# Attention scores' third partial product on 128 rows with zeros under the keys' low part; the last matrix and the value projections move 512 weight columns

## The chip, the cores and the metric

The kernel runs on one core of a Trainium2 chip. The metric is device time in microseconds (us), as a median over runs. The engines are TensorE (PE in the profile, with its weight loads as PEld), VectorE (DVE), ScalarE (ACT), GpSimd (POOL) and SyncE (SP), which here only issues DMAs.

## The reference

The input is one sequence of 512 tokens with 1024 features. Two layers of a first block and then one layer of a second block are applied.

```python
# first block, each of 2 layers
h = rmsnorm(x, attn_norm)
a_q, a_k, a_v, b_q, b_ff, b_fb, b_i, b_g, gate_a, gate_b = split(h @ w_in)
y_a = diff_attention(a_q, a_k, a_v, ...) @ w_a     # 4 heads, 2 softmax maps of 64 dims each
y_b = hgrn2_bidirectional(b_q, ...) @ w_b          # 4 heads, gated scan over the tokens
x = x + (sigmoid(gate_a) * y_a + sigmoid(gate_b) * y_b) @ w_o
h = rmsnorm(x, ffn_norm)
x = x + (silu(h @ w_gate) * (h @ w_up)) @ w_down
# second block, 1 layer: local attention (8 heads of 64, 2 key heads), a state-space scan, and
f = square(relu(h @ w_ff_in)) @ w_ff_out           # 1024 -> 4096 -> 1024
x = x + rmsnorm(f, norm_mlp_post)
```

All values are 32-bit floats.

## The kernel before

**Products in three parts.** A large product is made from operands split into a high part (rounded to the fast 32-bit matmul type) and a low part (the rest). `mm3` (L224 to L227) issues three matmuls into the same PSUM bank: high by high, high by low, low by high. Weights come in chunks of 512 KB: `WChunk` (L203) issues one DMA on SP's queue into one of four buffers, and `wsplit` (L193) makes the parts of 512 columns when they are first used, the high part on ACT (L199), the low part on DVE (L200).

**Two orientations.** In `projA` the weights stand in the array (128 columns at a time) and all 512 tokens move through: each matmul has 512 moving columns. In `projV` (L637), which makes the values `va` and `vb` of the first block (two calls in each of two layers), and in `down` (L1538), the second block's last matrix, the tokens stand in the array, 128 at a time, and the weights move: there each matmul moves 256 weight columns. Two token tiles share one PSUM bank. `down(g)` for g = 0 to 3 takes a quarter of the 4096 hidden features each; it goes over four quarters `cq` of the output columns, for g = 3 over three, and `finish` does the last quarter token tile by token tile, with the final norm and the stores.

**Scores.** `stack_split` (L229) splits a projected query or key tile in two heads of 64 rows each. Of 128 array rows, 64 hold the high part and 64 the low part of the query (plane c of 2); for the keys both halves of plane c hold the high part, and a third plane holds the low parts of both heads. `mm_stacked` (L240) makes a pair of score tiles: for each c one matmul on 128 rows (L243: high by high plus low by high), and then for each c one on the 64 rows that hold the high parts of the query and the low parts of the keys (L246). It is called by `attn` (L719), four query tiles of each of the first block's eight heads with 512 keys, and by `local_attention` (L1174), 16 calls with 256 or 128 keys.

**Order of the work.** The Tile framework fixes each engine's order when the kernel is built: an instruction that is not ready in its planner's account is passed over and later work is taken. So in the first block matmuls of the next head's projections (`proj_h`, L680) stand in PE's order between the steps of `attn` and of `hgrn` (L760), the scan, whose levels go from PE (L775) over multiplications in `H` on POOL and DVE (L796) to a copy of the left keys on ACT (L677), and back to PE. In the second block matmuls of the gates' projections stand between the steps of the local attention.

**Where results leave PSUM.** There are three `mm` banks, two `at` banks and one each of `hg`, `tp` and `mi`. `projV` ends with eight ACT instructions (L657) of 256 columns; `down` with four a quarter, on ACT for g = 0 (L1552) and on DVE after that (L1554).

**The start.** `FirstNorm.start` (L363) issues the input's loads with the first weight chunks of `projV` between them.

Of the kernel before, what the change touches and what calls it, by code (L numbers as in the profile page):

```python
# [11 lines left out]
F32 = mybir.dt.float32  # L12
# [59 lines left out]
def model_kernel(ctx: ExitStack, tc: tile.TileContext, I, O, dbg=None):  # L72
# [155 lines left out]

    def stack_split(src, dst):  # L229

        keys = dst.shape[1] == 3
        for c in range(2):
            own, other = slice(c * 64, c * 64 + 64), slice(64 - c * 64, 128 - c * 64)
            A.activation(out=dst[own, c, :], in_=src[own, :], func=AF.Copy)
            if keys:
                A.activation(out=dst[other, c, :], in_=src[own, :], func=AF.Copy)
            V.tensor_tensor(out=dst[own, 2, :] if keys else dst[other, c, :], in0=src[own, :], in1=dst[own, c, :],
                            op=ALU.subtract)

    def mm_stacked(pss, q, k):  # L240

        for c in range(2):
            PE.matmul(out=pss[c], lhsT=q[:, c, :], rhs=k[:, c, :], start=True, stop=False)  # L243
        for c in range(2):
            own = slice(c * 64, c * 64 + 64)
            PE.matmul(out=pss[c], lhsT=q[own, c, :], rhs=k[own, 2, :], start=False, stop=True)  # L246

    def projA(W, c0, nm, xsf, K=8, kbase=0, loader=None, hooks=None):

# [71 lines left out]
    class Norm:  # L321
# [8 lines left out]
        def on(self, m, x):  # L330
            sc = {} if self.pre is None else {"scale": self.pre[:, m:m + 1]}
            if self.n == 0:
                A.activation(out=self.ss, in_=x, func=AF.Square, **sc)
            else:
                sq = stile([128, 512], "sq", bufs=2)
                A.activation(out=sq, in_=x, func=AF.Square, **sc)  # L336
                if self.n < 7 or not self.short:
                    P.tensor_tensor(out=self.ss, in0=self.ss, in1=sq, op=ALU.add)  # L338
                else:
                    self.parts.append(sq)  # L340
            self.n += 1
# [18 lines left out]
    class FirstNorm:  # L360


        def start(self, ah, va, vb, Win):  # L363
            self.xt = [ah.tile([128, 4, 512], F32, name="H4", tag="H4", bufs=2) for _ in range(2)]
            self.xm = [va[:, m, :] for m in range(4)] + [vb[:, m, :] for m in range(4)]
            self.ah, pre = ah, {}
            for q in range(4):
                nc.sync.dma_start(out=self.xt[q // 2][:, :, q % 2 * 256:q % 2 * 256 + 256],
                                  in_=I["x"][0, :, q * 256:q * 256 + 256].rearrange("(t p) c -> p t c", p=128))
                if q % 2 == 0:  # L370
                    pre[(0, q // 2)] = WChunk(Win, 0, 4, 1024 + q // 2 * 256, 256)

            wm = ah.tile([128, 512], F32, name="e", tag="e", bufs=3)
            V.memset(wm, 0.0)
            A.activation(out=wm[0:1, 0:1], in_=mhalf[0:1, 0:1], func=AF.Copy)
            gps = mi_ps()
            for _ in range(WARM):
                PE.matmul(out=gps[:, 0:256], lhsT=wm[:, 128:256], rhs=wm[:, 256:512], start=True, stop=True)
            PE.transpose(gps[:, 0:8], prow0, ident[0:8, 0:8])
            self.g0 = stile([128, 8], "g0", bufs=1)  # L380
            V.tensor_copy(out=self.g0, in_=gps[:, 0:8])
            for m in range(4):
                self.tile(m)
                if m % 2:
                    pre[(0, 0)](m - 1, slice(0, 256))
            return pre

        def tile(self, m):
# [242 lines left out]
    def heads(l, Win, nrm, oA, oB, op_, ah):  # L631
# [3 lines left out]
        vb = ah.tile([128, 4, 512], F32, name="vb")  # L635

        def projV(c0, dst, hooks=None, pre={}):  # L637
            banks = [[mm_ps(), mm_ps()], [mm_ps(), at_ps()]]
            for k0 in (0, 4):
                for cc in range(2):  # L640
                    pss = banks[cc]
                    w = pre.get((k0, cc)) or WChunk(Win, k0, 4, c0 + cc * 256, 256)
                    for ka in (0, 2):
                        for t in range(4):
                            o = pss[t // 2][:, (t % 2) * 256:(t % 2) * 256 + 256]
                            for k in (ka, ka + 1):
                                xh, xl = xs(k0 + k)
                                ts_ = slice(t * 128, (t + 1) * 128)
                                wh, wl = w(k, slice(0, 256))
                                mm3(o, xh[:, ts_], xl[:, ts_], wh, wl,  # L650
                                    k0 + k == 0 and t % 2 == 0, k0 + k == 7 and t % 2 == 1)
                    if hooks is not None:
                        next(hooks, None)
            rcol = nrm.cols
            for cc in range(2):
                for t in range(4):
                    A.activation(out=dst[:, t, cc * 256:cc * 256 + 256],  # L657
                                 in_=banks[cc][t // 2][:, (t % 2) * 256:(t % 2) * 256 + 256],
                                 func=AF.Copy, scale=rcol[:, t:t + 1])

        def proj_rope(c0, tag):
            mark("proj_" + tag)
# [4 lines left out]
            V.tensor_tensor(out=t1, in0=ps, in1=Crs, op=ALU.mult)  # L667
            P.tensor_tensor(out=sh, in0=sh, in1=Srs, op=ALU.mult)
            V.tensor_tensor(out=t1, in0=t1, in1=sh, op=ALU.add)
            dst = ah.tile([128, 2 if tag == "aq" else 3, 512], F32R, name=tag, tag=tag, bufs=2)  # L670
            stack_split(t1, dst)
            return dst

# [500 lines left out]
    def local_attention(lp, oL, kvp):  # L1174
# [17 lines left out]
        pad(lp, 992)  # L1192
        kt = lp.tile([128, 512], F32, name="kt", tag="kt", bufs=1)
        V.tensor_tensor(out=kt, in0=kvp[0], in1=rbc, op=ALU.mult)
        kh = lp.tile([128, 3, 512], F32R, name="kh")
        stack_split(kt, kh)
        vt = lp.tile([128, 512], F32, name="vt", tag="kt", bufs=1)
        V.tensor_tensor(out=vt, in0=kvp[1], in1=rbc, op=ALU.mult)
# [116 lines left out]
    with ExitStack() as mst:  # L1315
# [78 lines left out]
        with ExitStack() as st:  # L1394
# [20 lines left out]
                            m == 0 and k == 0, m == 1 and k == 7)  # L1415

            def evac(hs, p, ps):
                sq = stile([128, 512], "sq", bufs=2)
                A.activation(out=sq, in_=ps[p], func=AF.Square)
                for j in range(2):  # L1420
                    A.activation(out=yo[:, 4 + 2 * p + j, hsl(hs)], in_=ps[p][:, hsl(j)], func=AF.Copy,
                                 scale=gpost[4 + 2 * p + j])
                ss = pn.ss[:, hsl(hs)]
                if p == 1:
                    return [ss, sq[:, hsl(0)], sq[:, hsl(1)]]
                for j in range(2):
                    P.tensor_tensor(out=ss, in0=ss, in1=sq[:, hsl(j)], op=ALU.add)
# [55 lines left out]
    with ExitStack() as st:  # L1483
# [50 lines left out]
        def squares(t, cq):  # L1534
            jk = fp.tile([128, 256], F32, name="jk", tag="jk", bufs=2)
            A.activation(out=jk, in_=acc[:, t, cq * 256:cq * 256 + 256], func=AF.Square, accum_out=ssq[:, t, cq:cq + 1])

        def down(g):  # L1538
            for cq in range(4 if g < 3 else 3):
                pss = [mm_ps() for _ in range(2)]  # L1540
                csl = slice(cq * 256, cq * 256 + 256)
                for k0 in (0, 4):
# [5 lines left out]
                for t in range(4):  # L1548
                    o = pss[t // 2][:, (t % 2) * 256:(t % 2) * 256 + 256]
                    dst = acc[:, t, csl]  # L1550
                    if g == 0:
                        A.activation(out=dst, in_=o, func=AF.Copy, scale=r2[:, t:t + 1])  # L1552
                    else:
                        V.scalar_tensor_tensor(out=dst, in0=o, scalar=r2[:, t:t + 1], in1=dst, op0=ALU.mult, op1=ALU.add)  # L1554
# [77 lines left out]
```

## Time and profile before

| | us |
|---|---|
| median of 3 runs (2378.78 to 2381.04) | 2378.87 |
| the profiled execution | 2378.16 |
| its span on the core | 2376.4 |
| PE busy, share of the span | 2340.1, 98% |
| PEld busy | 1967.3, 83% |
| DVE busy | 1366.8, 58% |
| ACT busy | 1030.5, 43% |
| POOL busy | 448.2, 19% |

The profile is of one execution, 0.7 us under the median. 1.8 us of it lie outside the span. A matmul's duration in the rows includes the time in which its results leave the array, while the next one already runs: what one matmul costs is read from the distance between two starts and not from its duration. In a row of the timeline the columns are start, duration, engine, line, operation, tiles and shape, how many instructions are merged, and in brackets the engine's idle time before it with what ended that.

### The profile page before, as it was taken

How to read it: one execution, taken by the hardware profiler on the slowest of the kernel's cores; microseconds unless marked ns; L12 is line 12 of the kernel's file. 1: busy time of each engine (PE TensorE's matmuls, PEld its weight loads, DVE VectorE, ACT ScalarE, POOL GpSimd, SP SyncE). 2: the span in 40 equal slices, each digit the busy share in tenths (PEclk: the TensorE clock that was granted, in tenths of full speed). 3: DMA queues.
4: the chain of work that ended last, by engine and by line, in shares of the span. 5: the costliest groups of instructions: out<-in, count | busy, mean ns of one | idle time of the engine just before them, and what ended most of it. 6: DMA issues, size and time to landing. Idle time of an engine off the chain costs nothing.

```text
span 2376.4 us, 32220 instructions
## 1 busy us (share of the span) xinstructions
PE 2340.1 (98%) x12207; PEld 1967.3 (83%) x12207; DVE 1366.8 (58%) x2370; ACT 1030.5 (43%) x1936; POOL 448.2 (19%) x754
## 2 busy tenths in 40 slices
PE   9999999999999999999999999999999999999998
PEld 9877788888888897777888888888776788898998
DVE  5777755554444547777556544445766875434444
ACT  6566644433232335566434332323356354533232
POOL 0122210170151311222101726100300102000002
PEclk9999999999999999999999999999999999999999
DMA  6211124333333432111243333333433543233231
GB/s 224 71 54 54 54 71 160 106 103 105 106 101 106 130 116 72 54 48 60 66 131 106 110 113 106 107 107 92 125 97 107 169 142 98 83 96 98 89 98 63
DMA packets 252539, 237.53 MB, mean 100 GB/s; under 512 B 18936, under 2 KB 237640, under 8 KB 252384
## 3 DMA queue, kind: packets, MB, share of 16 engines
q1 hardware_dynamic: 232992, 204.81, 28.4%
q10 hardware_dynamic: 15584, 21.33, 2.8%
q0 software_dynamic: 3808, 9.33, 1.3%
q8 instruction: 96, 1.57, 0.3%
q14 instruction: 59, 0.48, 0.1%
HBM read 216.42 MB, written 20.59 MB: 100 GB/s over the span
## 4 chain that ended last, share of the span: by engine, by line
PE 87%; DVE 7%; ACT 2%; issue 2%; DMA 1%; POOL 1%; ACTq 0%; DVEq 0%; POOLq 0%
PE mm L225 24%; PE mm L227 24%; PE mm L226 24%; PE hg L775 2%; PE at L246 1%; PE at L243 1%; DVE hT L800 1%; PE at L227 1%; PE at L225 1%; PE at L226 1%; DVE wlo L200 1%; PE mi L750 1%; PE tp L744 1%; PE hg L1254 1%; POOL H L796 0%
## 5 line engine op out<-in xcount | busy, mean ns | idle before, releaser
L200 DVE TENSOR_TENSOR wlo<-wraw,whi 128x512 fp32r<-128x512 f32 x736 | 536.6, 733 | 706.3 <-ACT whi L199 683.3
L199 ACT ACTIVATE whi<-wraw 128x512 fp32r<-128x512 f32 x736 | 458.6, 629 | 891.6 <-PE mm L226 665.3
L225 PE MATMUL mm<-xg,whi 128*128 128x512 f32 (+1 forms) x1736 | 679.8, 392 | 1.6 <-DVE dt L905 1.6
L226 PE MATMUL mm<-xg,whi 128*128 128x512 f32 (+1 forms) x1736 | 676.3, 390 | 1.3 <-DVE xg L1436 1.2
L227 PE MATMUL mm<-xg,wlo 128*128 128x512 f32 (+1 forms) x1736 | 676.4, 390 | 0.0
L227 PEld LDWEIGHTS mm<-xg,wlo 128*128 128x128 f32 x1736 | 326.7, 188 | 69.4 <-issue 4.8
L225 PEld LDWEIGHTS mm<-xg,whi 128*128 128x128 f32 x1736 | 327.0, 188 | 67.9 <-issue 3.4
L226 PEld LDWEIGHTS mm<-xg,whi 128*128 128x128 f32 x1736 | 327.0, 188 | 67.8 <-issue 2.7
L226 PE MATMUL mm<-wlo,a 128*128 128x256 f32 x512 | 144.9, 283 | 0.0
L227 PE MATMUL mm<-whi,a 128*128 128x256 f32 x512 | 144.9, 283 | 0.0
L225 PE MATMUL mm<-whi,a 128*128 128x256 f32 x512 | 144.9, 283 | 0.0
L225 PE MATMUL mm<-a,whi 128*128 128x512 f32 x352 | 137.2, 390 | 0.6 <-DVE dt L905 0.6
L226 PE MATMUL mm<-a,whi 128*128 128x512 f32 x352 | 136.9, 389 | 0.0
L227 PE MATMUL mm<-a,wlo 128*128 128x512 f32 x352 | 136.9, 389 | 0.0
L338 POOL TENSOR_TENSOR ss<-ss,sq 128x512 f32<-128x512 f32 x36 | 54.1, 1510 | 372.3 <-ACT sq L336 371.6
L796 POOL TENSOR_TENSOR H<-H,hT 128x512 f32<-128x512 f32 x56 | 65.2, 1165 | 225.6 <-PE hg L775 148.1
L225 PEld LDWEIGHTS mm<-whi,a 128*128 128x128 f32 x512 | 98.3, 192 | 0.1
L226 PEld LDWEIGHTS mm<-wlo,a 128*128 128x128 f32 x512 | 98.3, 192 | 0.1
L227 PEld LDWEIGHTS mm<-whi,a 128*128 128x128 f32 x512 | 98.3, 192 | 0.0
L225 PEld LDWEIGHTS mm<-a,whi 128*128 128x128 f32 x352 | 66.1, 188 | 14.9 <-DVE dt L905 1.0
L227 PEld LDWEIGHTS mm<-a,wlo 128*128 128x128 f32 x352 | 66.1, 188 | 13.7
L226 PEld LDWEIGHTS mm<-a,whi 128*128 128x128 f32 x352 | 66.1, 188 | 13.7
(491 smaller groups left out, 3829.5 us busy)
## 6 DMA issues: line engine op xcount, KB each, us to landing
wraw<-in_w_in_dram SPq DMA_DIRECT2D x118, 512.0 KB, 3.7
wraw<-in_w_gate_dram SPq DMA_DIRECT2D x44, 512.0 KB, 3.6
wraw<-in_w_up_dram SPq DMA_DIRECT2D x44, 512.0 KB, 3.8
wraw<-in_w_down_dram SPq DMA_DIRECT2D x40, 512.0 KB, 3.4
wraw<-in_w_ff_in_dram SPq DMA_DIRECT2D x32, 512.0 KB, 3.7
wraw<-in_w_ff_out_dram SPq DMA_DIRECT2D x32, 512.0 KB, 3.4
wraw<-in_w_o_dram SPq DMA_DIRECT2D x16, 512.0 KB, 3.6
xT<-xd SPq DMA_DIRECT2D x24, 256.0 KB, 5.0
```

The source lines that it names most:

```text
L199: A.activation(out=hi[:, :n], in_=raw, func=AF.Copy)
L200: V.tensor_tensor(out=lo[:, :n], in0=raw, in1=hi[:, :n], op=ALU.subtract)
L225: PE.matmul(out=ps, lhsT=ah, rhs=bh, start=first, stop=False)
L226: PE.matmul(out=ps, lhsT=ah, rhs=bl, start=False, stop=False)
L227: PE.matmul(out=ps, lhsT=al, rhs=bh, start=False, stop=last)
L243: PE.matmul(out=pss[c], lhsT=q[:, c, :], rhs=k[:, c, :], start=True, stop=False)
L246: PE.matmul(out=pss[c], lhsT=q[own, c, :], rhs=k[own, 2, :], start=False, stop=True)
L338: P.tensor_tensor(out=self.ss, in0=self.ss, in1=sq, op=ALU.add)
L744: PE.transpose(tp[:, b * 128:(b + 1) * 128], es[0][:, b * 128:(b + 1) * 128], ident)
L750: PE.matmul(out=o[:, i * 128:(i + 1) * 128], lhsT=wT[:, b * 128:(b + 1) * 128], rhs=va[:, b, h * 128:(h + 1) * 128], start=b == 0, stop=b ...
L775: PE.matmul(out=ps[:, sl].rearrange("p (n two h) -> p n two h", two=2, h=hh), lhsT=KT[:, sl], rhs=halves(H4, 1, 2, hh, b * 128, 128), star ...
L796: eng.tensor_tensor(out=tgt, in0=tgt, in1=mul.unsqueeze(3).to_broadcast([128, 2, nb, hh]), op=ALU.mult)
```

## The change

1. `stack_split` gives the keys four planes. Plane 2 + c holds the low part of head c on its own 64 rows, and zeros on the other 64, written by a `memset` on POOL (two for each of the nine key tiles).
2. `mm_stacked` makes the third product on 128 rows, right behind the first one of the same c, with the same stationary tile.
3. The scratch tile `sq` of the norms moves from the pool that lives through the kernel to the pool of the residual stream; the two key buffers of the first block are 2 KB larger each.
4. `projV` moves 512 columns: chunks of two rows of tiles by 512 columns (512 KB, as before), one PSUM bank for each token tile, four ACT instructions of 512 columns at the end. `FirstNorm.start` loads the first two of these chunks at the same places in the queue.
5. `down(0)` to `down(2)` and the first half of `down(3)` move 512 columns (`down_half`): columns 0 to 511 into the banks `at`, `at`, `tp`, `mi`, columns 512 to 1023 into the three `mm` banks and `hg`. The third quarter of `down(3)` and `finish` stay as they were.

```diff
     def stack_split(src, dst):
-        keys = dst.shape[1] == 3
+        keys = dst.shape[1] == 4
...
             if keys:
                 A.activation(out=dst[other, c, :], in_=src[own, :], func=AF.Copy)
-            V.tensor_tensor(out=dst[own, 2, :] if keys else dst[other, c, :], in0=src[own, :], in1=dst[own, c, :],
+                P.memset(dst[other, 2 + c, :].bitcast(F32), 0.0)
+            V.tensor_tensor(out=dst[own, 2 + c, :] if keys else dst[other, c, :], in0=src[own, :], in1=dst[own, c, :],
                             op=ALU.subtract)
     def mm_stacked(pss, q, k):
         for c in range(2):
             PE.matmul(out=pss[c], lhsT=q[:, c, :], rhs=k[:, c, :], start=True, stop=False)
-        for c in range(2):
-            own = slice(c * 64, c * 64 + 64)
-            PE.matmul(out=pss[c], lhsT=q[own, c, :], rhs=k[own, 2, :], start=False, stop=True)
+            PE.matmul(out=pss[c], lhsT=q[:, c, :], rhs=k[:, 2 + c, :], start=False, stop=True)
...
-                sq = stile([128, 512], "sq", bufs=2)
+                sq = cur["xp"].tile([128, 512], F32, name="sq", tag="sq", bufs=2)
...
-                    pre[(0, q // 2)] = WChunk(Win, 0, 4, 1024 + q // 2 * 256, 256)
+                    pre[q] = WChunk(Win, q, 2, 1024, 512)
...
         def projV(c0, dst, hooks=None, pre={}):
-            banks = [[mm_ps(), mm_ps()], [mm_ps(), at_ps()]]
-            for k0 in (0, 4):
-                for cc in range(2):
...
+            banks = [mm_ps(), mm_ps(), mm_ps(), at_ps()]
+            for k0 in range(0, 8, 2):
+                w = pre.get(k0) or WChunk(Win, k0, 2, c0, 512)
+                for k in range(2):
+                    xh, xl = xs(k0 + k)
+                    wh, wl = w(k, slice(0, 512))
+                    for t in range(4):
+                        ts_ = slice(t * 128, (t + 1) * 128)
+                        mm3(banks[t], xh[:, ts_], xl[:, ts_], wh, wl, k0 + k == 0, k0 + k == 7)
+                if hooks is not None:
+                    next(hooks, None)
...
+            for t in range(4):
+                A.activation(out=dst[:, t, :], in_=banks[t], func=AF.Copy, scale=rcol[:, t:t + 1])
...
+        def down_half(g, ch):
+            pss = [at_ps(), at_ps(), tp_ps(), mi_ps()] if ch == 0 else [mm_ps(), mm_ps(), mm_ps(), hg_ps()]
+            csl = slice(ch * 512, ch * 512 + 512)
+            for k0 in range(0, 8, 2):
+                w = WChunk(W2, g * 8 + k0, 2, ch * 512, 512)
+                for k in range(2):
+                    for t in range(4):
...
+                        mm3(pss[t], a[:, 0, tsl], a[:, 1, tsl], wh, wl, k0 + k == 0, k0 + k == 7)
+            for t in range(4):
+                evac(g, t, csl, pss[t])
...
         def down(g):
-            for cq in range(4 if g < 3 else 3):
+            down_half(g, 0)
+            if g < 3:
+                down_half(g, 1)
+                return
+            for cq in (2,):
```

## Rows read from the trace of the kernel before

**Rows 1.** The page's first part: busy time, share and instructions of an engine.
```profile
PE   2340.1 (98%) x12207; PEld 1967.3 (83%) x12207; DVE 1366.8 (58%) x2370; ACT 1030.5 (43%) x1936; POOL 448.2 (19%) x754
```

**Rows 2.** Groups by line and shape on PE: columns as in the page's part 5.
```profile
L225 PE MATMUL mm<-whi,a 128*128 128x256 f32 x512 | 144.9, 283 | 0.0
...
L225 PE MATMUL mm<-whi,xg 128*128 128x256 f32 x192 | 54.5, 285 | 0.1
...
L225 PE MATMUL at<-whi,xg 128*128 128x256 f32 x64 | 18.1, 283 | 0.0
```

**Rows 3.** Timeline of PE in `down(0)`, 256 moving columns.
```profile
2110.23 0.28 PE L225 MATMUL mm<-whi,a 128*128 128x256 f32 x1
...
2111.19 0.28 PE L227 MATMUL mm<-whi,a 128*128 128x256 f32 x1
```

**Rows 4.** Timeline of PE in the projection after it, 512 moving columns.
```profile
2150.22 0.39 PE L225 MATMUL mm<-xg,whi 128*128 128x512 f32 x1
...
2150.90 0.39 PE L225 MATMUL mm<-xg,whi 128*128 128x512 f32 x1
```

**Rows 5.** The 64-row matmuls by shape: one line's view.
```profile
L246 PE MATMUL at<-ak,aq x64: 491/498/502, 92.6 to 1129.7; 64*128 64x512 f32 x64
...
L246 PE MATMUL at<-kh,qh x32: 322/380/384, 1745.9 to 1804.6; 64*128 64x256 f32 x24, 64*128 64x128 f32 x8
```

**Rows 6.** Timeline of PE: a scores call whose 64-row matmuls stand alone.
```profile
218.61 0.39 PE L243 MATMUL at<-ak,aq 128*128 128x512 f32 x1
218.92 0.50 PE L246 MATMUL at<-ak,aq 64*128 64x512 f32 x1
219.35 0.50 PE L225 MATMUL mm<-xg,whi 128*128 128x512 f32 x1
219.69 0.39 PE L243 MATMUL at<-ak,aq 128*128 128x512 f32 x1
```

**Rows 7.** Timeline of PE: a call whose two 64-row matmuls stand together.
```profile
225.34 0.94 PE L243 MATMUL at<-ak,aq 128*128 128x512 f32 x2
226.21 0.50 PE L246 MATMUL at<-ak,aq 64*128 64x512 f32 x2
226.65 0.50 PE L227 MATMUL mm<-xg,wlo 128*128 128x512 f32 x1
```

**Rows 8.** Timeline of PE: the first call of a head.
```profile
212.18 0.50 PE L243 MATMUL at<-ak,aq 128*128 128x512 f32 x1 [0.31 <-DVE aq L237]
212.90 0.50 PE L243 MATMUL at<-ak,aq 128*128 128x512 f32 x1 [0.22 <-DVE aq L237]
```

**Rows 9.** Timeline of PE: a call of the local attention, 256 keys.
```profile
1760.26 0.28 PE L243 MATMUL at<-kh,qh 128*128 128x256 f32 x1
...
1761.74 0.27 PE L1249 MATMUL tp<-ident,lg 128*128 128x128 f32 x1
```

**Rows 10.** Timeline of ACT: copies of the left keys in a head's scan.
```profile
231.72 0.62 ACT L677 COPY hKT<-H 128x512 f32<-128x512 f32 x1 [1.47 <-DVE amx L732]
...
239.57 0.62 ACT L677 COPY hKT<-H 128x512 f32<-128x512 f32 x1 [1.31 <-DVE arc L738]
```

**Rows 11.** Timeline of PE: the scan's matmuls that read those copies.
```profile
232.64 1.05 PE L775 MATMUL hg<-H,hKT 128*128 128x128 f32 x8
```

**Rows 12.** The same, without a scores call since the level before.
```profile
240.24 1.16 PE L775 MATMUL hg<-H,hKT 128*128 128x128 f32 x8 [0.18 <-ACT hKT L677]
```

**Rows 13.** Windows: L225 alone, a head's stretch with its scan; PE busy and count first.
```profile
213.76:249.18 35.42, 8.36 (x20) 3.78 (x20) 1.00 0.15 46
```

**Rows 14.** POOL, groups by shape: one input, 512 columns.
```profile
L1045 POOL TENSOR_SCALAR Z<-BA,cf 128x512 f32<-128x512 f32 x8 | 12.6, 1589 | 0.4
```

**Rows 15.** A `memset` of 512 columns on DVE, one line's view.
```profile
L374 DVE MEMSET e<- x1: 485/485/485, 1.2 to 1.2; 128x512 f32 x1
```

**Rows 16.** DVE, groups by shape: a result of 512 columns read from PSUM.
```profile
L394 DVE SCALAR_TENSOR_TENSOR xg<-at,g,xg 128x512 fp32r<-128x512 f32 x2 | 1.5, 748 | 1.1 <-ACT xg L393 1.1
```

**Rows 17.** Timeline of ACT where layer 1's first `projV` ends.
```profile
34.62 1.28 ACT L438 ACT_TABLE_LOAD   x1
```

More of the change, by code (lines that the diff above doesn't have):

```diff
@@ L384, in start @@
                 if m % 2:
-                    pre[(0, 0)](m - 1, slice(0, 256))
+                    pre[0](m // 2, slice(0, 512))
             return pre
@@ L637, in projV @@
         def projV(c0, dst, hooks=None, pre={}):
-            banks = [[mm_ps(), mm_ps()], [mm_ps(), at_ps()]]
-            for k0 in (0, 4):
-                for cc in range(2):
[L641 to L653, printed above, removed]
-            rcol = nrm.cols
[L655 to L659, printed above, removed]
+            banks = [mm_ps(), mm_ps(), mm_ps(), at_ps()]
[9 more added lines that the diff above has]
+                    next(hooks, None)
+            rcol = nrm.cols
+            for t in range(4):
+                A.activation(out=dst[:, t, :], in_=banks[t], func=AF.Copy, scale=rcol[:, t:t + 1])
         def proj_rope(c0, tag):
@@ L669, in proj_rope @@
             V.tensor_tensor(out=t1, in0=t1, in1=sh, op=ALU.add)
-            dst = ah.tile([128, 2 if tag == "aq" else 3, 512], F32R, name=tag, tag=tag, bufs=2)
+            dst = ah.tile([128, 2 if tag == "aq" else 4, 512], F32R, name=tag, tag=tag, bufs=2)
             stack_split(t1, dst)
@@ L1194, in local_attention @@
         V.tensor_tensor(out=kt, in0=kvp[0], in1=rbc, op=ALU.mult)
-        kh = lp.tile([128, 3, 512], F32R, name="kh")
+        kh = lp.tile([128, 4, 512], F32R, name="kh")
         stack_split(kt, kh)
@@ L1417, in evac @@
             def evac(hs, p, ps):
-                sq = stile([128, 512], "sq", bufs=2)
+                sq = cur["xp"].tile([128, 512], F32, name="sq", tag="sq", bufs=2)
                 A.activation(out=sq, in_=ps[p], func=AF.Square)
@@ L1536, in squares, with evac @@
             A.activation(out=jk, in_=acc[:, t, cq * 256:cq * 256 + 256], func=AF.Square, accum_out=ssq[:, t, cq:cq + 1])
-        def down(g):
-            for cq in range(4 if g < 3 else 3):
+        def evac(g, t, csl, o):
+            dst = acc[:, t, csl]
+            if g == 0:
+                A.activation(out=dst, in_=o, func=AF.Copy, scale=r2[:, t:t + 1])
+            else:
+                V.scalar_tensor_tensor(out=dst, in0=o, scalar=r2[:, t:t + 1], in1=dst, op0=ALU.mult, op1=ALU.add)
+        def down_half(g, ch):
[5 more added lines that the diff above has]
+                    for t in range(4):
+                        a = acts[g * 8 + k0 + k]
+                        tsl = slice(t * 128, (t + 1) * 128)
+                        wh, wl = w(k, slice(0, 512))
+                        mm3(pss[t], a[:, 0, tsl], a[:, 1, tsl], wh, wl, k0 + k == 0, k0 + k == 7)
+            for t in range(4):
+                evac(g, t, csl, pss[t])
+                if g == 3:
+                    for cq in (2 * ch, 2 * ch + 1):
+                        squares(t, cq)
+                    P.tensor_tensor(out=acc[:, t, csl], in0=acc[:, t, csl], in1=gpb[:, csl], op=ALU.mult)
+        def down(g):
+            down_half(g, 0)
[3 more added lines that the diff above has]
+            for cq in (2,):
                 pss = [mm_ps() for _ in range(2)]
@@ L1550, in down @@
                     dst = acc[:, t, csl]
[L1551 to L1554, printed above, removed]
+                    evac(g, t, csl, o)
                     if g == 3:
```

## The prediction

> **What bounds the kernel now.** I read the page's first part, then PE's groups by shape, then PE's timeline. The page shows PE busy 98% of the span with more weight loads and matmuls than any engine has instructions [rows 1]. So the question for each edit is what it does to the distance between PE's starts, and whether PE then waits for something else. The timeline gives that distance, since a duration covers the way out of the array too. A matmul of 256 moving columns follows the one before it after 0.120 us: 8 steps from 2110.23 to 2111.19 [rows 3]. One of 512 takes 0.227: 3 steps in 0.68 [rows 4]. Two narrow ones cost 0.240, one wide one 0.227: each instruction costs 13 ns beside its columns.
>
> The second thing to see is what happens around a 64-row matmul. There are 96: 64 with 512 columns, 24 with 256, 8 with 128 [rows 5]. Where one stands alone, it starts 0.31 us after the 128-row matmul before it, the next one 0.43 after that, and the one after that 0.34 later [rows 6]. At 0.227 each, three steps are 0.68; they take 1.08. So 0.40 us is lost at each. The Trainium skill, "TensorEngine Tiling (Array Packing)", section "Key Properties", says that changing the tiling mode, not just the tile, drains the engine; the trace agrees, by those 0.40 us.
>
> **Part A, 512 weight columns.** The narrow matmuls of `down` are 512 in each of three forms, those of `projV` 192 + 64 in each [rows 2], so 1536 and 768. Of `down`'s, 96 stay for the third quarter of g = 3 and 96 in `finish`. 1344 + 768 = 2112 become 1056, and each pair gives 13.3 ns (0.240 less 0.68/3): 14.1 us. Columns, high and low splits and their work on ACT and DVE stay the same, and so do the number, size and place of the weight DMAs on SP's queue; a split of 512 columns now serves 12 matmuls of 0.227 (2.72 us) instead of 24 of 0.120 (2.88 us), so it must come 6% sooner.
>
> What can take some of it back is the end of a group. Before, half of the banks were done half a group early; now four banks are done in the last 2 us, 0.68 us apart, and the next projection wants the first at once and the second 1.36 us later. This happens at six places: after four `projV` calls (ACT) and after `down(0)` and `down(1)` (DVE). The first bank is done 2.04 us before the group's end and read in about 0.75 us [rows 16], so 1.3 us are left for whatever stands before it on that engine. The worst thing seen there is a table load of 1.28 us on ACT, behind the end of the first `projV` [rows 17]. The bound is 0 to 1.3 us for each; I take 0.25, nearer to nothing since one such load just fits: 1.5 us. Part A nets 12.6 us. The half of `down(3)` goes into banks that nobody wants after it, and the end of the kernel (third quarter, `finish`) is not touched: nothing.
>
> **Part B, scores on 128 rows.** In the first block each head has four calls. In two of them the 64-row matmuls stand alone, as in [rows 6]: 8 heads with 4 alone, 32 in all, at 0.40: 12.8 us. In the other two calls of a head they stand together, and these two run beside each other: both begin at about 226.21, and the next instruction starts 0.44 later [rows 7], which is no less than two wide matmuls one after the other (0.453). The drain before (0.31 less 0.227, 0.09) and the load after (0.34 less 0.227, 0.11) remain, less the 0.01: 0.19 for each of 16 pairs, 3.0 us. At the first call of a head the second matmul waits for the query's split, 0.72 us behind the first [rows 8]; in the new order the third product of c = 0 lies in that wait: 0.227 for 8 heads, 1.8 us. Heads: 17.6 us.
>
> In the local attention a call with 256 keys takes from 1760.26 to 1761.74, with one projection matmul in it [rows 9]: 1.48 against 4 x 0.120 + 0.227 = 0.71. That is 0.77 for 12 calls, 9.2 us. The four calls with 128 keys I estimate between a pair (0.19) and this (0.77), at 0.4: 1.6 us. Local: 10.8. Part B gross: 28.4 us.
>
> How much arrives? Freed PE time is lost if the next instruction in PE's fixed order waits for another chain. In the scan, a copy of the keys ends at 231.72 + 0.62 = 232.34 [rows 10] and PE reads it at 232.64 [rows 11]: 0.30 us to spare, with one lone 64-row matmul (0.40) since the level before. At a level without a call the copy ends at 240.19 and PE is there at 240.24 [rows 10, 12]: it waits for it. So the spare time is about what the calls cost PE, and without that cost PE comes just in time rather than early. I charge 0.3 us a head, 2.4, and in the local attention, whose chains over DVE and ACT are denser, a quarter, 2.7 (between nothing and all 10.8; my choice, as most of its steps have projection matmuls in front). Part B nets 23.3 us.
>
> **Small edits.** Two POOL memsets for each of nine key tiles, 64 x 512: a row of 512 columns costs 0.49 us on DVE [rows 15] and at most 1.6 on POOL [rows 14]; so 1 to 3.2 us a head on POOL. Behind them on POOL stand the query's rotation and the scan's multiplications. They are covered since the keys are made one projection (24 x 0.227 = 5.4 us) before the query, and the memset waits for no data. If that cover failed, a head would lose up to 3.2 us (26 in all, in the range's upper end in part). The scratch tile `sq` moves 4 KB without adding an instruction: nothing. The loads at the start keep size and place: nothing.
>
> **Sum.** Profiled execution 2378.16 (span 2376.4 and 1.8 outside) less 12.6 less 23.3 is 2342.3; the median lies 0.7 above the profiled one: 2343.
>
> **Rivals.** (1) *The freed time in the calls is waited out.* The order on PE stays, and the scan's and the softmax's chains set the pace. For it: PE waits already at levels without a call [rows 12]. Against it: the spare time before the others [rows 10, 11]. With three quarters of part B lost: 2378.9 - 12.6 - 7.1 = 2359. (2) *The 64-row products were cheap.* A pair of them works in the array at once, and two products on 128 rows replace one slot by two. If the gaps around them were due to something that stays, 32 pairs at 0.227, 12 at 0.120 and 4 at some 0.11 would be added, 9.1 us: 2378.9 - 12.6 + 9.1 = 2375. The same page of the Trainium skill, in "When to Use Tiling", advises two-fold row tiling for a contraction of 64, and so speaks against this change; the trace speaks against the rule here, since a pair takes 0.44. (3) *The order gets worse, and it is slower.* In a head's 35 us of scan some 60 projection matmuls (20 from each of three lines) stand between the chain's steps [rows 13]. The order is made anew at each build. If a third of them fell out of that stretch (20 x 0.227 = 4.5 us a head, 36 in all), by three wide banks held longer or by memsets ahead of the scan, the whole gain would be gone, and with half of them it is 2378.9 - 35.9 + 54 = 2397. Nothing in the rows points there, but nothing excludes it.
>
> **How the numbers follow.** The forecast has 0.80, with its own range of 2334 (all of A and B, 42.5 less, and a little more) to 2353; rival 1 has 0.12, rival 2 has 0.03, rival 3 has 0.05. The range reaches from 2334 to rival 1's 2360. About 0.2% (4.8 us) is what a measurement here can tell from no change. Faster: forecast and rival 1, 0.92. Same: rival 2, 0.03. Slower: rival 3, 0.05.
>
> **What would show it.** In the profile after, `down` and `projV` should show L225 to L227 with 512 columns, 0.227 us apart, and 1056 fewer matmuls. L246 should be gone, and in a call four starts 0.227 apart, with the next matmul at 0.227 too. Wrong would be: steps of 0.3 or more in these calls (rival 2); idle time before L775, L744 or L1249 that was not there (rival 1); fewer projection matmuls in a head's scan (rival 3); a wait for ACT or DVE at the first matmul behind `projV` or `down` of more than 1.3 us; a wait for POOL before the scores.

## The result and the profile after

The changed kernel takes 2349.71 us (median of 4, 2348.67 to 2351.14), the kernel before 2378.82 us beside it: a ratio of 0.9877 (95% interval 0.9860 to 0.9894). That is 29.1 us less; the sum had 35.9. The time lies in the range, and the sign and the likeliest case came true, but one term of the sum was wrong by ten microseconds.

The profile after has a span of 2347.3 us, 29.1 less than before. Part 1 of its page, against [rows 1]:

```profile
PE 2301.5 (98%) x11151; PEld 1912.0 (81%) x11151; DVE 1369.9 (58%) x2350; ACT 1029.2 (44%) x1912; POOL 460.1 (20%) x768
```

PE has 1056 matmuls fewer (12207 less 11151), as counted, and its share still reads 98%: the share doesn't tell that something new is waited for. The groups by shape, which answer to [rows 2]:

```profile
L225 PE MATMUL mm<-whi,xg 128*128 128x512 f32 x96 | 38.2, 398 | 0.4 <-ACT whi L199 0.4
...
L225 PE MATMUL mm<-whi,a 128*128 128x512 f32 x72 | 28.0, 389 | 0.0
...
L225 PE MATMUL mm<-whi,a 128*128 128x256 f32 x64 | 18.1, 283 | 0.0
```

What is left of 256 columns in `down` is the third quarter of g = 3 and `finish`. The view of the first score line, which answers to [rows 5] (L245 has the same shapes and counts):

```profile
L244 PE MATMUL at<-ak,aq x64: 389/474/504, 89.5 to 1120.4; 128*128 128x512 f32 x64
...
L244 PE MATMUL at<-kh,qh x32: 220/282/387, 1735.8 to 1785.7; 128*128 128x256 f32 x24, 128*128 128x128 f32 x8
```

Its last row gives the length of the local attention's scores, 1735.8 to 1785.7. In [rows 5] it is 1745.9 to 1804.6: nine of the 29 us lie there. The other stages were measured in the same way, from the start of one matmul to the start of another in PE's timeline of either kernel:

| stage | before | after | difference | gross in the prediction |
|---|---|---|---|---|
| `projV`, layer 1 (its first to its last matmul) | 49.03 | 46.53 | -2.50 | -2.55 |
| heads, layer 1 (first scores to first `w_a` matmul) | 251.99 | 249.68 | -2.31 | -8.8 |
| `projV`, layer 2 | 48.23 | 47.54 | -0.69 | -2.55 |
| heads, layer 2 | 254.54 | 251.59 | -2.95 | -8.8 |
| local attention (first to last scores) | 58.94 | 49.96 | -8.98 | -10.8 |
| first `down` matmul to the end | 278.38 | 269.39 | -8.99 | -8.94 |
| all the rest | 1435.3 | 1432.6 | -2.7 | 0 |

So the loss is in the heads: 5.3 us arrived of 17.6. The scores calls there did become what was planned. PE's timeline in a head, which answers to [rows 6]:

```profile
213.48 0.39 PE L244 MATMUL at<-ak,aq 128*128 128x512 f32 x1
213.71 0.39 PE L245 MATMUL at<-ak,aq 128*128 128x512 f32 x1
213.93 0.39 PE L225 MATMUL mm<-xg,whi 128*128 128x512 f32 x1
214.16 0.39 PE L244 MATMUL at<-ak,aq 128*128 128x512 f32 x1
214.39 0.39 PE L245 MATMUL at<-ak,aq 128*128 128x512 f32 x1
214.62 1.13 PE L766 MATMUL hg<-H,hKT 128*128 128x128 f32 x8
```

All starts are some 0.23 us apart. (From `projV` on, lines are 9 lower than before: L775 is now L766, L744 is L735, L739 is L730, L796 is L787.) What changed beside that stands in the view of PE's waits for the stretch from 100 to 300 us, three and a third heads. Its columns are what waited for what, us in total, times, the longest. First the kernel before, then the changed one:

```profile
PE at L243 <- DVE aq L237: 2.2, 6, 1.0
PE hg L809 <- POOL H L796: 1.5, 3, 0.8
PE hg L775 <- ACT hKT L677: 0.5, 3, 0.2
```

```profile
PE tp L735 <- DVE e L732: 5.2, 8, 1.1
PE at L244 <- DVE aq L238: 2.2, 3, 1.1
PE hg L766 <- ACT hKT L668: 1.9, 8, 0.3
PE hg L774 <- DVE H L787: 1.1, 4, 0.3
```

4.2 us of waits became 10.4. The new one is the first: the transposes of the softmax weights (L735) wait for VectorE's combination of the two maps (L732), up to 1.1 us once in a head. One such place in the changed kernel, on DVE, POOL and PE:

```profile
219.97 0.17 DVE L729 RECIPROCAL arc<-als 128x2 f32<-128x2 f32 x1 [1.37 <-ACT e L725]
220.18 0.99 DVE L730 TENSOR_TENSOR arc<-arc,nlam 128x1 f32<-128x1 f32 x1
221.09 0.72 DVE L768 COPY_PREDICATED hWd<-cm,hg 128x512 f32<-128x512 uint8 x1
221.70 0.73 DVE L732 SCALAR_TENSOR_TENSOR e<-e,arc 128x512 f32<-128x512 f32 x1
...
219.99 1.16 POOL L787 TENSOR_TENSOR H<-H,hT 128x512 f32<-128x512 f32 x1 [2.65 <-ACT e L725]
...
219.60 0.47 PE L244 MATMUL at<-ak,aq 128*128 128x512 f32 x1
...
222.58 0.63 PE L735 MATMUL tp<-ident,e 128*128 128x128 f32 x4 [1.10 <-DVE e L732]
```

L730 multiplies one number in each partition. It takes 0.99 us, begins 0.19 us behind a multiplication of the scan on POOL, and ends with it (221.17 and 221.15). Beside no POOL instruction it takes 0.15. In the kernel before the same instruction stands later against POOL's:

```profile
225.74 1.16 POOL L796 TENSOR_TENSOR H<-H,hT 128x512 f32<-128x512 f32 x1 [2.62 <-ACT e L734]
...
225.76 0.17 DVE L738 RECIPROCAL arc<-als 128x2 f32<-128x2 f32 x1 [1.37 <-ACT e L734]
225.84 0.74 DVE L777 COPY_PREDICATED hWd<-cm,hg 128x512 f32<-128x512 uint8 x1
226.48 0.43 DVE L739 TENSOR_TENSOR arc<-arc,nlam 128x1 f32<-128x1 f32 x1
...
227.44 0.74 DVE L741 SCALAR_TENSOR_TENSOR e<-e,arc 128x512 f32<-128x512 f32 x1
...
228.32 0.63 PE L744 MATMUL tp<-ident,e 128*128 128x128 f32 x4
```

There it again ends with POOL's (226.91 and 226.90), but only 0.42 us of that were left. Both happen in 8 of the 32 calls, once in each head. The Trainium skill, "SBUF — State Buffer", section "SBUF: two separate sides", says that VectorE and GpSimd share one pair of ports as an exclusive lock: a VectorE instruction with two inputs in SBUF and a GpSimd instruction that reads SBUF don't run beside each other, and the later one stands still until the first has ended. The trace agrees, by 0.99 and 0.43 against 0.15 us.

The longer L730 does not make this chain longer, however. From the start of the reciprocal to the end of the combination it takes 2.42 us in the kernel before (225.76 to 228.18) and 2.46 in the changed one (219.97 to 222.43), as VectorE does its work there in another order. What changed is PE. Before, it comes to the transposes 0.14 us behind the combination, after the two 64-row products and six projection matmuls; in the changed kernel it has had no 64-row products and only three projection matmuls to do there (the others stand elsewhere), and is idle for 1.10 us. From the first matmul of the scores call that stands before them to the transposes it is 2.98 us in both (from 225.34 in [rows 7], and from 219.60).

### The profile page after: what moved, and what is told of

Same layout as the page of the kernel before. It is cut to its first block, busy times and chain, and to the rows that moved or that the text cites. A ratio compares the mean times of both kernels' runs of the same rounds, so it can differ in the third digit from the quotient of the medians.

```text
span 2347.3 us, 30081 instructions
## 1 busy us (share of the span) xinstructions
PE 2301.5 (98%) x11151; PEld 1912.0 (81%) x11151; DVE 1369.9 (58%) x2350; ACT 1029.2 (44%) x1912; POOL 460.1 (20%) x768
## 4 chain that ended last, share of the span: by engine, by line
PE 82%; DVE 10%; ACT 3%; issue 3%; DMA 1%; POOL 1%; ACTq 0%; DVEq 0%; POOLq 0%
PE mm L225 22%; PE mm L226 22%; PE mm L227 22%; DVE H L787 2%; PE hg L766 1%; PE at L225 1%; PE at L227 1%; PE at L226 1%; DVE hWd L768 1%; DVE e L732 1%; DVE hT L791 1%; DVE wlo L200 1%; ACT hKT L668 1%; PE at L244 1%; PE hg L225 1%
## 5 line engine op out<-in xcount | busy, mean ns | idle before, releaser
L225 PE MATMUL mm<-xg,whi 128*128 128x512 f32 (+1 forms) x1736 | 678.7, 391 | 1.6 <-DVE dt L896 1.6
L225 PEld LDWEIGHTS mm<-xg,whi 128*128 128x128 f32 x1736 | 327.2, 188 | 66.4 <-DVE dt L896 2.0
L225 PE MATMUL mm<-a,whi 128*128 128x512 f32 x352 | 137.2, 390 | 0.6 <-DVE dt L896 0.6
L787 POOL TENSOR_TENSOR H<-H,hT 128x512 f32<-128x512 f32 x56 | 66.8, 1193 | 217.9 <-PE hg L766 122.4
L225 PEld LDWEIGHTS mm<-a,whi 128*128 128x128 f32 x352 | 66.1, 188 | 14.8 <-DVE dt L896 1.0
L227 PEld LDWEIGHTS mm<-a,wlo 128*128 128x128 f32 x352 | 66.1, 188 | 13.8
L225 PE MATMUL mm<-mrg,whi 128*128 128x512 f32 (+1 forms) x208 | 75.9, 365 | 0.0
L226 PE MATMUL mm<-mrg,whi 128*128 128x512 f32 (+1 forms) x208 | 75.8, 365 | 0.0
L227 PE MATMUL mm<-mrg,wlo 128*128 128x512 f32 (+1 forms) x208 | 75.8, 365 | 0.0
L766 PEld LDWEIGHTS hg<-H,hKT 128*128 128x128 f32 x448 | 59.1, 191 | 12.7 <-ACT hKT L668 10.6
L1553 POOL TENSOR_TENSOR acc<-acc,gpb 128x512 f32<-128x512 f32 x4 | 5.5, 1406 | 322.4 <-ACT jk L1527 322.4
L766 PE MATMUL hg<-H,hKT 128*128 128x128 f32 x448 | 64.8, 288 | 3.7 <-ACT hKT L668 3.7
```

What stands on the lines that cost most here:

```text
L225: PE.matmul(out=ps, lhsT=ah, rhs=bh, start=first, stop=False)
L226: PE.matmul(out=ps, lhsT=ah, rhs=bl, start=False, stop=False)
L227: PE.matmul(out=ps, lhsT=al, rhs=bh, start=False, stop=last)
L766: PE.matmul(out=ps[:, sl].rearrange("p (n two h) -> p n two h", two=2, h=hh), lhsT=KT[:, sl], rhs=halves(H4, 1, 2, hh, b * 128, 128), star ...
L787: eng.tensor_tensor(out=tgt, in0=tgt, in1=mul.unsqueeze(3).to_broadcast([128, 2, nb, hh]), op=ALU.mult)
```

## The experiments

The theory after these readings: in the heads the chains of the softmax and the scan over VectorE and ScalarE come last, not PE; the 64-row matmuls stood in time in which PE would otherwise have waited; and VectorE's instructions that stand still beside GpSimd's make these chains long. The rivals: the 64-row matmuls were cheap; the two parts of the change hinder each other; the new order alone is at fault.

**One part alone: the 512 columns.** The changed kernel with the three-plane keys and the 64-row products of before.

```diff
...
-            PE.matmul(out=pss[c], lhsT=q[:, c, :], rhs=k[:, 2 + c, :], start=False, stop=True)
+        for c in range(2):
+            own = slice(c * 64, c * 64 + 64)
+            PE.matmul(out=pss[c], lhsT=q[own, c, :], rhs=k[own, 2, :], start=False, stop=True)
...
```

> The changed kernel with the scores as they were (64-row third products, keys in three planes); only the 512 weight columns are new. By the trace of the changed kernel, the stages with wide weights gave 2.4 us in layer 1's value projections, 0.7 in layer 2's and 9.0 in the last matrix. Theory (both parts are independent): 12 us less than before, 2367. Rival (part of the loss in the heads comes from the wide projections, whose order the planner changed as well): under 2364 or over 2370, with head periods other than before's 60 to 61 us.

Measured: 2364.79 us (2362.83 to 2366.48), ratio 0.9942 (0.9925 to 0.9959): 13.8 us less than before. Part A gives its 14.1 gross nearly whole.

**The other part alone: the 128-row scores.** The kernel before with the new `stack_split`, `mm_stacked` and `sq`, and 256 columns in `projV` and `down`.

```diff
...
-        for c in range(2):
-            own = slice(c * 64, c * 64 + 64)
-            PE.matmul(out=pss[c], lhsT=q[own, c, :], rhs=k[own, 2, :], start=False, stop=True)
+            PE.matmul(out=pss[c], lhsT=q[:, c, :], rhs=k[:, 2 + c, :], start=False, stop=True)
...
```

> The kernel before with the scores' third product on 128 rows and nothing else (the scratch tile sq moves with it, for room). Theory: the local attention gives about 10.8 us, the eight heads only 4 to 6 of the 17.6 us that the 64-row products cost there, since PE then waits for the softmax and the scan: 2362 to 2364. Rival (the heads lost their gain through the wide projections): 2350 to 2353.

Measured: 2363.25 us (2361.40 to 2365.46), ratio 0.9937 (0.9922 to 0.9951): 15.4 us less. 13.8 and 15.4 are 29.2, the changed kernel has 29.1: the parts don't hinder each other. The multiplication of one number takes 0.99 to 1.00 us in eight calls here too, and 0.43 to 0.44 in the run before, with the old scores: it comes with part B.

**64 rows again, in the order of after.** Every engine's instructions stand as in the changed kernel; only the third product reads its own 64 rows.

```diff
-            PE.matmul(out=pss[c], lhsT=q[:, c, :], rhs=k[:, 2 + c, :], start=False, stop=True)
+            own = slice(c * 64, c * 64 + 64)
+            PE.matmul(out=pss[c], lhsT=q[own, c, :], rhs=k[own, 2 + c, :], start=False, stop=True)
```

> The changed kernel with its order of issue in the scores, its four key planes and its memsets, but the third product reads only the 64 rows of its head. Theory (a change between 128 and 64 rows drains the array, 0.40 us for each of 96 products that stand alone): in the local attention some 10 us more, in the heads less than the 64 x 0.40 = 26 us because PE waits there anyway; 2362 to 2380. Rival (64-row products are cheap, the order made the gain): 2346 to 2353.

Measured: 2372.33 us (2370.14 to 2374.56), ratio 0.9975 (0.9965 to 0.9985), 22.6 us over the changed kernel. In this order the 64-row form costs 13.5 us in the heads and 9.7 in the local attention. In the heads some 2.6 us of that are two stretches of lower granted clock (an estimate, from the lengths of heads with and without one; see the end), so 10.9: the products were not cheap. But all 64 of them stand alone in this order, each between two matmuls of 128 rows, and at the prediction's 0.40 us each that would be 25.6. The place shown above, in PE's timeline of this run (it is 5.72 us later in the span):

```profile
225.32 0.48 PE L244 MATMUL at<-ak,aq 128*128 128x512 f32 x1
225.74 0.49 PE L246 MATMUL at<-ak,aq 64*128 64x512 f32 x1
226.16 0.50 PE L244 MATMUL at<-ak,aq 128*128 128x512 f32 x1
226.59 0.50 PE L246 MATMUL at<-ak,aq 64*128 64x512 f32 x1
227.02 0.50 PE L225 MATMUL mm<-xg,whi 128*128 128x512 f32 x1
...
228.30 0.63 PE L736 MATMUL tp<-ident,e 128*128 128x128 f32 x4 [0.32 <-DVE e L733]
```

From the first scores matmul to the transposes it is 228.30 - 225.32 = 2.98 us, with two 64-row products alone and a wait of 0.32. In the changed kernel it is 222.58 - 219.60 = 2.98 us, with none and a wait of 1.10. Here part B gained nothing: the chain over VectorE sets the end, and the time around the 64-row products stood in its shadow. The small multiplication takes 1.12 to 1.14 us here, longer than in the changed kernel, and PE waits less.

With 64 rows the heads are 8.2 us longer in this order than in the kernel before, 5.6 without the stretches of lower clock. That is no sign that the order of the other engines got worse: in the kernel before 32 of the products stand alone and 32 in 16 pairs, 15.8 us at the prediction's prices against the 25.6 here, and PE's waits over both layers' heads add up to 12 us there, 13 here and 23 in the changed kernel.

**The small multiplication with one input from a tile.** L730 takes `nlam` as a scalar operand.

```diff
-                V.tensor_tensor(out=r[:, 1:2], in0=r[:, 1:2], in1=nlam[:, l:l + 1], op=ALU.mult)
+                V.tensor_scalar(out=r[:, 1:2], in0=r[:, 1:2], scalar1=nlam[:, l:l + 1], scalar2=None, op0=ALU.mult)
```

> The changed kernel; the multiplication of the softmax's second reciprocal by minus lambda (one number a row, line 730 in the changed kernel) reads lambda as a scalar operand, so that the VectorE instruction has one tensor input, not two. In the changed kernel it took 0.99 us where it began 0.2 us behind a GpSimd multiplication and ended with it, against 0.15 us alone, and the transposes that need its result made PE wait 1.28 us in each head. Theory (two tensor inputs on VectorE wait for GpSimd's tensor instruction): it takes 0.2 us everywhere, the wait at line 735 falls by about 0.85 us a head, and the time by 4 to 7 us, to 2343 to 2346. Rival (the wait is the chain of the softmax itself): it still takes 0.9 us or PE waits as long in another place, 2349 to 2351.

Measured: 2346.90 us (2345.89 to 2347.09), ratio 0.9867 (0.9852 to 0.9881): 2.8 us less than the changed kernel, a little short of what was expected. The instruction takes 0.20 to 0.22 us in all calls. But the order came out otherwise, and it no longer stands behind POOL's multiplication; that this form doesn't stand still is not shown. PE's waits from 100 to 300 us:

```profile
PE hg L800 <- POOL H L787: 2.3, 3, 0.8
PE at L244 <- DVE aq L238: 2.0, 3, 1.0
PE hg L774 <- DVE H L787: 1.3, 4, 0.3
PE tp L735 <- DVE e L732: 1.2, 4, 0.3
PE hg L766 <- ACT hKT L668: 0.8, 4, 0.2
```

The wait at L735 fell from 5.2 to 1.2, and the scan's own last level (L800) is late now instead: 7.6 us remain of 10.4.

**The softmax's scale later.** The first map is scaled at the output, four ACT instructions a head, and VectorE makes the ratio of the two maps in one instruction.

```diff
...
-                V.tensor_tensor(out=r[:, 1:2], in0=r[:, 1:2], in1=nlam[:, l:l + 1], op=ALU.mult)
-                A.activation(out=es[0], in_=es[0], func=AF.Copy, scale=r[:, 0:1])
+                V.tensor_scalar(out=r[:, 1:2], in0=r[:, 1:2], scalar1=ls[:, 0:1], scalar2=nlam[:, l:l + 1],
+                                op0=ALU.mult, op1=ALU.mult)
...
-            A.copy(out=oA[:, h, :], in_=o)
+            for i in range(4):
+                A.activation(out=oA[:, h, i * 128:i * 128 + 128], in_=o[:, i * 128:i * 128 + 128], func=AF.Copy,
+                             scale=rs[:, i, 0:1])
```

> The changed kernel; in the first block's attention the two softmax maps are combined as e0 + (ratio) e1, with one VectorE instruction that makes the ratio, and the scale of the first map is applied when the output leaves PSUM. So one ScalarE instruction of 0.72 us is gone from the chain between scores and transposes in each of 32 calls, and the small multiplication with minus lambda has one tensor input. Theory (PE's waits in the heads are the softmax chain's, lengthened by the multiplication that stands behind GpSimd): the waits of 1.28 and 0.36 us before the transposes go, and the time falls by 4 to 9 us below the changed kernel's, to 2341 to 2346. Rival (the scan's chain sets the pace): the waits move to the scan's matmuls, 2347 to 2351.

Measured: 2348.63 us (2345.98 to 2351.21), ratio 0.9870 (0.9856 to 0.9885): not to be told from the changed kernel. The theory of the time fell: 7.9 us of waits remain, now mostly at the scan's levels: shortening the softmax's chain in this way brought nothing, as the scan's comes right behind it.

**The second layer's norm later.** The hook of the norm in `projV` runs one chunk later in layer 2, against the wait there (below).

```diff
-                if hooks is not None:
+                if hooks is not None and (l == 0 or k0 > 0 or dst is vb):
```

> The changed kernel; in layer 2's first value projection the sum of the norm's squares is asked for one weight chunk (5.4 us) later. In the changed kernel PE waits 1.16 us for GpSimd there (0.85 before), does eight short matmuls, and then the granted clock is 0.54 for 3.7 us. Theory (the wait is worth its length, and the low clock follows from it): no wait, full clock in that stretch, 1.2 to 3 us less, 2346.7 to 2348.5. Rival (it is made up elsewhere): 2349 to 2350.5.

Measured: 2348.79 us (2347.10 to 2349.86), ratio 0.9869 (0.9853 to 0.9886). `projV` of layer 2 is 2.8 us shorter than in the changed kernel, whose own stretch of lower clock there is gone, but a stretch of lower clock stands in the last head instead, and the total can't be told from the changed kernel's.

**GpSimd out of the scan.** Both halves of the multiplications in `H` on VectorE; the small multiplication keeps its two inputs.

```diff
-                    eng = P if half == 0 and hh > 1 else V
+                    eng = V
```

> The changed kernel with both halves of the scan's multiplications in H on VectorE, none on GpSimd; the multiplication with minus lambda keeps its two tensor inputs. Theory (VectorE's instruction with two tensor inputs waited for GpSimd's): it takes 0.15 to 0.16 us in all 32 calls, and VectorE's half of the H multiplications 0.7 instead of 1.2 us. Rival (0.99 us is the instruction's own): eight calls stay at 0.99. The time may go either way, since VectorE gets 56 more multiplications of 0.7 us: 2343 to 2354.

Measured: 2325.48 us (2323.99 to 2326.24), ratio 0.9772 (0.9758 to 0.9787): 24.2 us less than the changed kernel, far more than expected. The groups of these multiplications, in the changed kernel and then in this one:

```profile
L787 DVE TENSOR_TENSOR H<-H,hT 128x512 f32<-128x512 f32 x56 | 54.9, 980 | 2.1 <-PE hg L774 1.4
L787 POOL TENSOR_TENSOR H<-H,hT 128x512 f32<-128x512 f32 x56 | 66.8, 1193 | 217.9 <-PE hg L766 122.4 <-ACT e L725 58.7 <-ACT whi L199 20.7
```

```profile
L787 DVE TENSOR_TENSOR H<-H,hT 128x512 f32<-128x512 f32 x112 | 72.3, 680 | 5.2 <-PE hg L774 5.2
```

Shared, the two halves took 0.98 and 1.19 us a piece; VectorE alone does one in 0.68, so twice the work costs it 17 us more in the whole kernel and spares POOL 67. The small multiplication, in the changed kernel and then here (shortest, median and longest in ns):

```profile
L730 DVE TENSOR_TENSOR arc<-arc,nlam x32: 149/160/1010, 95.7 to 1126.6; 128x1 f32<-128x1 f32 x32
```

```profile
L730 DVE TENSOR_TENSOR arc<-arc,nlam x32: 148/152/160, 97.0 to 1103.6; 128x1 f32<-128x1 f32 x32
```

So the 0.99 came from GpSimd. The chain at the place shown above, from the reciprocal to the combination, takes 2.07 us here instead of 2.46. All engines have a new order as well, so how much of the 24.2 us is the end of standing still and how much the order was not separated. In the window from 100 to 300 us PE doesn't wait at all (over both layers' heads 2.4 us of 23 are left). Its columns: us, then busy time and count of PE, PEld, DVE, ACT and POOL, granted clock, DMA share, GB/s; first the kernel before, then the changed kernel, then this one:

```profile
100.00:300.00 200.00, 195.60 (x1080) 157.25 (x1078) 154.29 (x290) 122.77 (x260) 48.13 (x41) 1.00 0.17 51
```

```profile
100.00:300.00 200.00, 189.61 (x1085) 157.96 (x1084) 159.29 (x288) 124.58 (x262) 51.24 (x46) 1.00 0.17 51
```

```profile
100.00:300.00 200.00, 200.00 (x1172) 169.86 (x1171) 164.91 (x326) 129.33 (x281) 21.07 (x20) 1.00 0.18 54
```

**The cross test: the same edit in the kernel before.** What is the 64-row form worth where GpSimd no longer holds VectorE up? Its edit:

```diff
-                    eng = P if half == 0 and hh > 1 else V
+                    eng = V
```

> The kernel before, with one edit: both halves of the scan's H multiplications on VectorE, none on GpSimd (the same edit that took the changed kernel from 2349.7 to 2325.5 us). Theory: in the heads VectorE's instructions that stand still beside GpSimd's multiplications ate the gain of the 128-row scores; with GpSimd out of it TensorE sets the pace in the heads with either form of the scores, so the old 64-row form should cost there what the prediction's sum gave gross, 17.6 us (15 to 20) against the changed kernel with the same edit, instead of the 5.3 us seen. With 13.8 us for the 256-column matmuls and 10.9 us for local attention that makes 2325.5 + 17.6 + 13.8 + 10.9 = 2368 us (2364 to 2371), and the two-input multiplication of 128x1 takes about 0.15 us in all 32 calls. Rival: VectorE and ScalarE set the pace of the heads even without GpSimd; then the heads differ by about 5 us again, and the time is 2352 to 2358 us.

Measured: 2366.82 us (2366.63 to 2367.83), ratio 0.9950 (0.9936 to 0.9963), within the theory's 2364 to 2371 and outside the rival's. The heads, from the first scores to the first `w_a` matmul, take 248.7 and 247.5 us here and 235.5 and 239.3 in the run before: 21.5 us for part B, somewhat over the expected 15 to 20 and four times the 5.3 seen with GpSimd in. The order differs here too: 48 of the 64-row products stand alone and 16 in 8 pairs, which at the prediction's prices is 20.7 us. So the gross price does arrive once GpSimd is out of the scan. The edit itself brought 12 us with the old scores (in the heads 10.3) and 24.2 with the new ones: each change uncovers the other.

**The best version.** The scan on VectorE and the norm one chunk later, in the changed kernel.

```diff
-                if hooks is not None:
+                if hooks is not None and (l == 0 or k0 > 0 or dst is vb):
...
-                    eng = P if half == 0 and hh > 1 else V
+                    eng = V
```

> The changed kernel with both halves of the H multiplications on VectorE and the second layer's norm hook one chunk later: two edits that were each run alone. Theory: the wait of about 1.2 us for the norm's sum in the second layer's projection goes, with the stretch of lower granted clock behind it, and nothing takes its place: 2322 to 2324.5 us against 2325.5. Rival: the stretch of lower clock only comes elsewhere, as it did when that edit was run alone: 2324.5 to 2327 us.

Measured: 2320.83 us (2320.44 to 2323.60), ratio 0.9760 (0.9747 to 0.9773): 58 us less than before and 29 less than the changed kernel. `projV` of layer 2 is 2.9 us shorter than in the run with the scan alone, with no stretch of lower clock. Of the 4.7 us between these two medians, 1.4 lie at the start in the two traces, which neither edit touches.

## Why the prediction was right, and which term was wrong

**Part A, right.** `down` had 672 pairs at 13.3 ns, 8.9 us, and 9.0 arrived; `projV` of layer 1 had 2.55 and 2.50 arrived. The charge of 0.25 us for each group's end was not needed: behind `down(0)` the next projection follows without a gap.

```profile
2121.20 0.39 PE L227 MATMUL hg<-whi,a 128*128 128x512 f32 x1
2121.42 0.39 PE L225 MATMUL mm<-xg,whi 128*128 128x512 f32 x1
```

`projV` of layer 2 lost 1.9 of its 2.55, not at its end but in its middle. PE's timeline there, and then the window behind the wait, whose last three columns are granted clock, DMA share and GB/s:

```profile
842.89 0.39 PE L227 MATMUL at<-whi,xg 128*128 128x512 f32 x1
844.27 1.05 PE L316 MATMUL mi<-inv,ss 128*128 128x1 f32 x8 [1.00 <-POOL ss L337]
...
846.25 0.63 PE L225 MATMUL mm<-whi,xg 128*128 128x512 f32 x1
846.68 0.63 PE L226 MATMUL mm<-wlo,xg 128*128 128x512 f32 x1
```

```profile
845.80:848.60 2.80, 2.80 (x8) 2.20 (x7) 1.78 (x4) 0.00 (x0) 1.24 (x1) 0.50 0.43 107
```

The norm's sum on POOL comes 1.0 us late, and then seven matmuls stand 0.43 apart instead of 0.227: 1.4 us. In the kernel before PE waits 0.7 us at the same place, so the hook within the group, which the prediction didn't cost, took 0.3 us. The rest is the stretch of lower clock: four other runs with the wide `projV` (the 512 columns alone, 64 rows again, one input, the scale later) have the same wait of 1.0 us and no such stretch, and there it takes 46.0 us, so that 2.25 of 2.55 arrive.

**Part B, the price of the 64-row matmuls, right.** With every engine's order kept, undoing the edit costs 22.6 us, and with GpSimd out of the scan 21.5 us in the heads alone, where 0.40 for a lone product and 0.19 for a pair make 20.7.

**Part B in the heads, wrong.** The step that failed is "I charge 0.3 us a head". 2.4 us were taken off 17.6; it should have been 12.3, 1.5 us a head. The spare time of 0.30 us [rows 10, 11] was read at one step, a copy of the scan, and taken for the spare time of all chains. At the transposes of each head's second call there was none. In the kernel before, the combination of the two maps ends at 228.18 and PE begins at 228.32; in the changed kernel, where PE waits for it, the same two are 222.43 and 222.58. So PE and the chain were level there already, and the 2.98 us from the scores to the transposes stayed. The prediction names idle time before L744 as a sign of rival 1, but read no row of that chain. By the view of PE's waits over both layers' heads they grew from 12.0 to 23.3 us, 11.3 of the missing 12.3; 10.4 of them stand before the transposes, where the view had none. With 64 rows in the same order those are 2.6 and all waits 13.1: the time around the 64-row products had hidden the rest.

So rival 1 (*the freed time in the calls is waited out*) came true in the heads alone: 70% of their gain was lost, close to its three quarters. Rival 3's mechanism had a small part: at the place shown three projection matmuls stand where six stood, but with 64 rows in the new order PE waits only 1.1 us more than in the kernel before. Rival 2 fell. That they were priced as cases for all of part B, and not stage by stage, is why their chances said little.

**Part B in the local attention, right.** 10.8 gross, 8.1 after the charge, 9.0 arrived; the view of PE's waits shows 0.4 us there. The chains that were called denser lost less than those that were thought easy.

**Small edits, right.** The 18 memsets (16 in the first block, two in the second) take 0.52 us each on POOL, and no engine waits for them.

```profile
L237 POOL MEMSET ak<- x16: 517/520/524, 2.1 to 1031.4; 64x512 f32 x16
```

**The account.** A gave 12.2 (12.6 forecast), the heads 5.3 (15.2), the local attention 9.0 (8.1). That A came so near is luck: its charge was not needed, and a stretch of lower clock took as much. The 2.7 us of the other stages are no gain that can be told: in the eleven traces these stages take between 1432.6 and 1436.3 us. That the time came into the range is owed to its width (to 2353 for the forecast alone), and in part to those 2.7 us and the local attention's 0.9.

## What to carry to other kernels

Before freed engine time is counted, every chain that the engine waits on in that stretch must be followed, not the one whose slack is nearest: what a slow instruction hid becomes a wait. To see what it hid, put the old instruction back into the new order, and count how it stands there, alone or in pairs, before its cost is compared. Look in the other engines' rows for a group whose longest duration is several times its median, as a tiny instruction that takes as long as a neighbour's large one was here the sign that it stood still; whether the chain got longer by it is another question, and here it had not. Splitting work between VectorE and GpSimd was here slower than leaving it all on VectorE, and the gain of one change showed in full only with the other made.

## What the hardware showed

A VectorE instruction on one number in each partition took 0.99 us instead of 0.15, as it stood behind a GpSimd instruction; the large multiplications took 0.98 in the mean instead of 0.68. A `COPY_PREDICATED` of 512 columns beside POOL's multiplication took 0.74 us (at 225.84), no longer than elsewhere (0.71 to 0.75 in all 56 of the kernel before).

Stretches in which the granted clock is 0.50 (the 1.2 GHz level, 512 columns 0.43 us apart) stand in every trace: within some 60 us before and after the local attention and in the last microseconds in all eleven, and beside that in a head, in layer 2's `projV` or nowhere else, from run to run. Where a stage can be compared with the same stage without one, it was 1.3 to 1.8 us longer (`projV` of layer 2: 47.5 against 46.0). Those at the very end cost nothing that can be seen: from the first `down` matmul on it is 269.4 us whatever their length. The one shown stands behind a wait of PE of 1.0 us, but the same wait in four other runs has none behind it, nor have the waits of 1.1 us in the heads of the changed kernel. What brings such a stretch on was not settled, nor how much of the spread between runs of one kernel is theirs.
